# A hybrid decoder block on one core: the value part of its expert mixer written in program order on all engines, with new load rules, gather table and ending

## The chip, the core and the metric

The kernel runs on one core of a Trainium2 chip. The core has a matrix engine (TensorE, in the profile PE, with its weight loads as PEld), a vector engine (VectorE, DVE), a scalar engine (ScalarE, ACT), a general one (GpSimd, POOL), and a queue engine (SyncE, SP) that only issues transfers here. SP, ACT and POOL issue transfers, and 16 DMA engines carry them. The metric is the device time of one launch in microseconds, the median of several runs.

## The reference

One layer of a decoder for 512 tokens of width 1024: sliding-window attention beside gated linear attention, and then a channel mixer that picks, for each token and each of 8 heads, 16 of 16384 experts by product keys. The change lies in this mixer alone:

```python
def block(args):
    xb, eb, gb = args
    ub = jnp.take(u, eb, axis=0)
    hid = jax.nn.gelu(jnp.einsum('tkd,td->tk', ub, xb), approximate=False) * gb
    vb = jnp.take(v, eb, axis=0)
    return jnp.einsum('tk,tkd->td', hid, vb)
```

`u` and `v` are 16384 x 1024 in float32 each. The block's output is scaled by a row (gate 2), added to the residual, and a final RMS norm with a weight row follows.

## The kernel before

Of the four blocks of 128 tokens three (`DENSE`, 384 tokens) go through all experts: gelu(h u^T) for all 16384, times a dense matrix of gates that is zero where an expert was not picked, times v. (Of the third block's tokens 32 have their hidden values gathered; so the u side has 352 columns.) The experts lie in 128 chunks of 128. A float32 matmul is made of three (`mm3`, L69 to L72): each operand is split into a high part (a copy on ScalarE, L65) and a low part (a subtraction on VectorE, L66), by `hilo`. The fourth block (`GB`) gathers its rows: for each of 128 picks, `gather_u` gathers 128 rows of u (512 KB, an indirect transfer issued by GpSimd, L994) and takes their dot with the tokens on VectorE (L1004); `gather_v` gathers the rows of v (L1021) and adds them to `gacc` with the gelu'd, gated dot as weight (L1026). `gather_to` walks one list of 256 gathers, of which 24 dots are made earlier.

A **u chunk** (`u_part`, L693) is 24 matmuls of 352 columns and a gelu on ScalarE. 84 chunks (`AHEAD`: all even ones, and the odd ones from 89) are made before, while the gates are computed, and their gelus are spilled to DRAM (`gsp`). The other 44, odd, are made in the V part. A **v chunk** (`v_part`, L1165) takes a pair of chunks of v (1 MB for two), the gates of 8 chunks (`gr`, 1.5 MB from `Gd` in DRAM, one load for 8 chunks), the gelu (back from DRAM, `gel`, or from the odd u chunk), multiplies gates and gelu on VectorE (L1185), splits the product (`Ah` on ScalarE, L1189; `Al` on VectorE, L1190) and v (`vh`, `vl`), and adds 18 matmuls of 512 columns into six accumulators, two for each of the three blocks.

The loop of the V part goes over c from 0 to 123: at an even c the u chunk c + 9 (if it is not made ahead), then the v chunk, then as many gathers as a running share (4.0 for c in a pair with a u, 2.3 without) asks for, until c = 121. The last four chunks are multiplied block by block, and `finish` (L1202) multiplies a block by gate 2, adds the residual, squares it, makes the root (L80 to L87), scales and stores; for `GB` this is done at c = 123.

**What sets the order.** Instructions of an engine run in the order in which they are built. A list scheduler with an estimated timeline sets that order, unless an engine is under a manual schedule: then the order of the program stands. In the V part before, GpSimd alone is manual; VectorE, ScalarE, TensorE and SP are the scheduler's. Tiles come from pools of a fixed number of places (five `gr` and two `gr2` for gathers, four high and four low parts, four `Ah` and `Al`, three `raw`, two `vraw`, two for the gates), and an instruction that writes a place waits until its last reader is done.

Of the kernel before, what the change touches and what calls it, by code (L numbers as in the profile page):

```python
# [47 lines left out]
def peer_block_kernel(ctx: ExitStack, tc: tile.TileContext, a: dict, out: bass.AP):  # L48
# [951 lines left out]
    def gather_u(s):  # L1000
# [4 lines left out]
        if s % 8 == 7:  # L1005
            sl = slice(s - 7, s + 1)
            last_gelu["hg"] = nc.scalar.activation(hg[:, sl], hid[:, sl], AF.Gelu)
            waiting.append(sl)
# [149 lines left out]
    LAST = 4  # L1158

    def gates_of(j):  # L1160
        gates_of.next = dn.tile([P, NGRP, CG, TG], F32, tag="gring", bufs=2, name=f"gr{j}")
        load = (nc.sync if j else nc.gpsimd).dma_start(gates_of.next.rearrange("p g c t -> p g (c t)"), Gd[j])
# [155 lines left out]
```

## Time and profile before

| | us |
|---|---|
| median of 3 runs | 1521.37 (1520.15 to 1524.9) |
| profiled execution, its own time | 1526.09 |
| its span (first to last instruction) | 1524.3 |
| TensorE busy | 1447.2 (95%) |
| VectorE busy | 1265.6 (83%) |
| ScalarE busy | 676.5 (44%) |
| GpSimd busy | 502.3 (33%) |
| moved by DMA | 431.63 MB, mean 283 GB/s |

A row of a group of instructions names the line, the engine, the operation, what is written and read, the count, and then busy time, mean of one in ns, idle time before them and what ended it. A row of the timeline begins with the start in us and the duration. In a row of waits stand the waiter, what it waited for, and the sum in us, the number and the longest. Matmuls overlap, so that a row's duration is longer than the distance of two starts. The V part lies from 781 us to the end.

### The profile page before, as it was taken

The page shows a single profiled execution, that of the slowest core. Times are in us where ns is not written, and L with a number is a line of the kernel's source. Part 1 is how long each engine was busy: PE and PEld are TensorE (multiplying, and loading weights), DVE is VectorE, ACT ScalarE, POOL GpSimd, SP SyncE. Part 2 cuts the span into 40 slices and gives each one's busy share as a digit, 9 for nine tenths or more (in the row PEclk, how much of TensorE's full clock was granted, in tenths as well). Part 3 has the DMA queues.
Part 4 walks back from the last instruction along what each step waited for, and adds up shares of the span by engine and source line. Part 5 has one row for each costly group of instructions (what it writes and reads, how often), then busy time and mean ns, then how long its engine had stood idle before and what let it go on. Part 6 is the DMA issues. An engine that isn't in the chain of part 4 may idle for free. (4 is left out here: it accounts for less than half of the span.)

```text
span 1524.3 us, 24545 instructions
## 1 busy us (share of the span) xinstructions
PE 1447.2 (95%) x9387; PEld 1286.5 (84%) x9387; DVE 1265.6 (83%) x2421; ACT 676.5 (44%) x1072; POOL 502.3 (33%) x362
## 2 busy tenths in 40 slices
PE   3999999899999999999997999999999999998995
PEld 3787877788999999999996888888888888776774
DVE  7578757689999999799938878888788889897996
ACT  5455576533344555556633333333333333333333
POOL 1000000145506443032323344343443445554540
PEclk9999999999999999999998999999999999999998
DMA  9253435453347999799999999899998989999992
GB/s 347 99 208 111 169 98 206 148 191 111 138 163 242 325 360 349 243 319 330 316 352 404 380 357 344 311 334 357 347 339 320 345 311 344 392 403 406 373 347 88
DMA packets 165558, 431.63 MB, mean 283 GB/s; under 512 B 11856, under 2 KB 83568, under 8 KB 153024
## 3 DMA queue, kind: packets, MB, share of 16 engines
q1 hardware_dynamic: 109280, 259.88, 47.5%
q0 software_dynamic: 42000, 154.00, 27.1%
q10 hardware_dynamic: 14160, 16.19, 3.0%
q8 instruction: 73, 1.20, 0.3%
q14 instruction: 45, 0.37, 0.1%
HBM read 385.48 MB, written 44.50 MB: 282 GB/s over the span
## 5 line engine op out<-in xcount | busy, mean ns | idle before, releaser
L994 POOL DMA_INDIRECT gu<-in_u_dram,ix_u x128 | 181.7, 1420 | 281.6 <-DVE gacc L1026 104.1
L1021 POOL DMA_INDIRECT gv<-in_vP_dram,ix_v x128 | 172.8, 1350 | 209.6 <-DVE gu L1004 115.5
L1189 ACT ACTIVATE Ah<-gr 128x384 fp32r<-128x384 f32 x128 | 67.0, 525 | 336.7 <-PE acc L71 310.0
L1026 DVE SCALAR_TENSOR_TENSOR gacc<-gv,hg,gacc 128x1024 f32<-128x1024 f32 x127 | 162.7, 1281 | 0.9 <-DMA gv<-in_vP_dram,ix_v 0.7
L1004 DVE SCALAR_TENSOR_TENSOR gu<-gu,h2n 128x1024 f32<-128x1024 f32 x128 | 155.5, 1220 | 5.4 <-DMA gu<-in_u_dram,ix_u 5.2
L1190 DVE TENSOR_TENSOR Al<-gr,Ah 128x384 fp32r<-128x384 f32 x128 | 71.0, 557 | 51.7 <-ACT Ah L1189 49.0
L960 POOL DMA_INDIRECT spr<-in_u_dram,spix x32 | 72.5, 2266 | 104.9 <-DVE spr L965 67.8
L706 ACT ACTIVATE ge<-ph 128x352 f32<-128x352 f32 x128 | 57.8, 451 | 106.4 <-PE ph L72 106.4
L1076 POOL IOTA iot<- 128x256 bf16 x1 | 1.5, 1540 | 284.3 <-DVE h2Tl L681 284.3
L921 ACT ACTIVATE gs<-pg 128x512 f32<-128x512 f32 x96 | 95.2, 1116 | 0.0
L912 DVE TENSOR_TENSOR o<-o,gp 128x3072 bf16<-128x3072 bf16 x48 | 84.0, 1754 | 0.0
L919 PE MATMUL pg<-o,o 128*128 128x128 bf16 x1152 | 73.6, 219 | 0.0
L919 PEld LDWEIGHTS <-o 128*128 128x128 bf16 x1152 | 66.3, 97 | 5.4
L896 DVE TENSOR_TENSOR o<-iot,t 128x2048 bf16<-128x2048 bf16 x48 | 58.4, 1222 | 11.4 <-PE pg L919 11.4
L1185 DVE TENSOR_TENSOR gr<-gel,gr 128x352 f32<-128x352 f32 x84 | 39.7, 519 | 5.9 <-DMA gel<-gsp 5.9
L218 DVE SCALAR_TENSOR_TENSOR macc<-wa,scs,macc 128x1024 f32<-128x1024 f32 x28 | 39.3, 1403 | 4.4 <-DMA wa<-in_w_ada_dram 4.2
L965 DVE SCALAR_TENSOR_TENSOR spr<-spr,xs 128x1024 f32<-128x1024 f32 x32 | 39.1, 1221 | 2.3 <-DMA spr<-in_u_dram,spix 2.3
L1185 DVE TENSOR_TENSOR gr<-ge,gr 128x352 f32<-128x352 f32 x44 | 22.7, 522 | 21.6 <-DMA gr<-Gd 12.4
L71 PE MATMUL pq<-h2Tl,wq_0h 128*128 128x512 f32 (+1 forms) x80 | 27.9, 349 | 1.2 <-DVE h2Tl L681 1.2
L70 PE MATMUL pq<-h2Th,wq_0h 128*128 128x512 f32 (+1 forms) x80 | 28.0, 352 | 1.0 <-ACT qha L759 1.0
L71 PE MATMUL pq<-h2Tl,wq_1h 128*128 128x512 f32 (+1 forms) x80 | 28.1, 352 | 0.0
L72 PE MATMUL pq<-h2Th,wq_1l 128*128 128x512 f32 (+1 forms) x80 | 28.0, 350 | 0.0
(2610 smaller groups left out, 5029.5 us busy)
## 6 DMA issues: line engine op xcount, KB each, us to landing
u<-in_uT_dram SPq DMA_DIRECT2D x64, 1024.0 KB
v<-in_vP_dram SPq DMA_DIRECT2D x63, 1024.0 KB
Gd<-gs SPq DMA_DIRECT2D x23, 1024.0 KB
gr<-Gd SPq DMA_DIRECT2D x15, 1536.0 KB
wa<-in_w_ada_dram SPq DMA_DIRECT2D x20, 1024.0 KB
gsp<-ge ACTq DMA_DIRECT2D x84, 176.0 KB
gel<-gsp SPq DMA_DIRECT2D x41, 352.0 KB
wi<-in_w_in_dram SPq DMA_DIRECT2D x9, 1024.0 KB
```

The lines of the kernel that those rows point to most:

```text
L896: nc.vector.tensor_tensor(o12.rearrange("p g s k r -> p (g s) k r"), iot[:, None].to_broadcast([P, 2 * H, P, 2]), trs[n][0][:, g0:g0 + H]. ...
L912: nc.vector.tensor_tensor(o2, o12[:, :, 1, None].to_broadcast([P, H, 3, P, 2]), gp3[:, g0:g0 + H, :, None].to_broadcast([P, H, 3, P, 2]), ...
L919: nc.tensor.matmul(pt[:, i, :], o12[:, g, 0, :, r], o2[:, g, m, :, r], start=(m == 0), stop=(m == 2))
L921: nc.scalar.activation(gs[:, :, t0 + 4 * f:t0 + 4 * f + 4].rearrange("p b a -> p a b"), pt, AF.Copy)
L960: nc.gpsimd.indirect_dma_start(out=sp[j], out_offset=None, in_=a["u"], in_offset=bass.IndirectOffsetOnAxis(ap=sp["ix"][:, j:j + 1], axis=0))
L994: nc.gpsimd.indirect_dma_start(out=ur, out_offset=None, in_=a["u"], in_offset=bass.IndirectOffsetOnAxis(ap=ix_u[:, s:s + 1], axis=0))
L1004: nc.vector.scalar_tensor_tensor(ur, ur, 1.0, h2n, op0=OP.mult, op1=OP.mult, accum_out=hid[:, s:s + 1])
L1021: nc.gpsimd.indirect_dma_start(out=vr, out_offset=None, in_=a["vP"], in_offset=bass.IndirectOffsetOnAxis(ap=ix_v[:, s:s + 1], axis=0))
L1026: nc.vector.scalar_tensor_tensor(gacc, vr, hg[:, s:s + 1], gacc, op0=OP.mult, op1=OP.add)
L1185: nc.vector.tensor_tensor(A[:, :NGU], ge, A[:, :NGU], OP.mult)
L1189: nc.scalar.activation(grp(Ah), A, AF.Copy)
L1190: nc.vector.tensor_tensor(grp(Al), A, grp(Ah), OP.subtract)
```

## The change

All engines are under the manual schedule in the V part, and the V part is written anew around a list of steps `xs` (u chunks and v chunks, in the order in which TensorE takes them; a u chunk stands 8 or 9 chunks ahead of its v chunk, as before). `prep(i)` does what VectorE and ScalarE have to do for step i, and is called two steps ahead of the step's matmuls. The gathers stand inside `prep`, between the copies and the subtraction, by a table `due` that weighs each u step with 1.867 and each v step up to chunk 121 with 1.367. `loads(i)`, at the end of `prep(i)`, issues on SP each load whose place is free by then in program order and whose step is at most 9 to 12 ahead; when the u chunks are done, the three `raw` places serve v too. The first gates' load is split over SP and GpSimd, and v0 and its gelu move from GpSimd to SP. There are eight places for gathers instead of seven. The last four chunks are multiplied block by block, the first block by both halves together, and the ending of each block is split into halves that are interleaved. The dots' gelu moves behind the copies of a step. The number of matmuls and their forms stay, and everything ahead of the V part is built in the same order as before.

VectorE in the late part, around the subtraction for v chunk 100 (`vc100l`); `gu` and `gacc<-gv` are gathers, `Al` the low part of a gate product. Before:

```order
L1004 SCALAR_TENSOR_TENSOR gu112_13362,hid_2439<-gu112_13362,h2n_2430 128x1024
L1026 SCALAR_TENSOR_TENSOR gacc_8931<-gv95_13392,hg_2440,gacc_8931 128x1024
L1004 SCALAR_TENSOR_TENSOR gu113_13424,hid_2439<-gu113_13424,h2n_2430 128x1024
L1190 TENSOR_TENSOR Al102_13936<-gr12_13531,Ah102_13935 128x384
L1026 SCALAR_TENSOR_TENSOR gacc_8931<-gv96_13427,hg_2440,gacc_8931 128x1024
L1004 SCALAR_TENSOR_TENSOR gu114_13457,hid_2439<-gu114_13457,h2n_2430 128x1024
L1026 SCALAR_TENSOR_TENSOR gacc_8931<-gv97_13491,hg_2440,gacc_8931 128x1024
L1190 TENSOR_TENSOR Al103_13966<-gr12_13531,Ah103_13965 128x384
L1026 SCALAR_TENSOR_TENSOR gacc_8931<-gv98_13523,hg_2440,gacc_8931 128x1024
L66 TENSOR_TENSOR vc100l_13862<-v100_13859,vc100h_13861 128x1024
L66 TENSOR_TENSOR vc101l_13897<-v100_13859,vc101h_13896 128x1024
```

and now:

```order
L1289 TENSOR_TENSOR gr12_13422<-geo99_13523,gr12_13422 128x22x16
L1044 SCALAR_TENSOR_TENSOR gacc_8930<-gv104_13823,hg_2440,gacc_8930 128x1024
L1298 TENSOR_TENSOR vc99l_13817<-v98_13489,vc99h_13816 128x1024
L1302 TENSOR_TENSOR Al99_13821<-gr12_13422,Ah99_13820 128x384
L1289 TENSOR_TENSOR gr12_13422<-gel100_13654,gr12_13422 128x22x16
L1014 SCALAR_TENSOR_TENSOR gu121_13855,hid_2439<-gu121_13855,h2n_2430 128x1024
L1298 TENSOR_TENSOR vc100l_13849<-v100_13555,vc100h_13848 128x1024
L1302 TENSOR_TENSOR Al100_13853<-gr12_13422,Ah100_13852 128x384
L1289 TENSOR_TENSOR gr12_13422<-geo101_13590,gr12_13422 128x22x16
L1044 SCALAR_TENSOR_TENSOR gacc_8930<-gv105_13887,hg_2440,gacc_8930 128x1024
L1014 SCALAR_TENSOR_TENSOR gu122_13890,hid_2439<-gu122_13890,h2n_2430 128x1024
L1298 TENSOR_TENSOR vc101l_13881<-v100_13555,vc101h_13880 128x1024
```

Before, seven gathers stand between the subtractions of chunks 99 and 100, and the subtractions of four chunks follow each other; now one or two gathers stand in each step, and the list is thirteen gathers further on.

ScalarE at the start of the V part. Before:

```order
L706 ACTIVATE ge9_9091<-ph9_9066 128x352
L65 ACTIVATE vc0h_9097<-v0_9095 128x1024
L65 ACTIVATE vc1h_9133<-v0_9095 128x1024
L65 ACTIVATE uc11h_9166<-u9_9060 128x1024
L65 ACTIVATE vc2h_9199<-v2_9197 128x1024
L1189 ACTIVATE Ah0_9104<-gr0_9093 128x384
```

and now:

```order
L1290 ACTIVATE vc0h_9054<-v0_8949 128x1024
L1293 ACTIVATE Ah0_9058<-gr0_8946 128x384
L706 ACTIVATE ge7_9088<-ph7_9063 128x352
L1290 ACTIVATE vc1h_9090<-v0_8949 128x1024
L1293 ACTIVATE Ah1_9094<-gr0_8946 128x384
L706 ACTIVATE ge9_9126<-ph9_9101 128x352
L1284 ACTIVATE uc11h_9128<-u9_8935 128x1024
```

TensorE takes u11 ahead of v0 before, and v0 and v1 ahead of u11 now; the copies follow that.

SP at the same place (`gr0` are the first gates, `gr1` the next). Before:

```order
L698 DMA u9_9060<-in_uT_dram 128x2048
L1171 DMA v2_9197<-in_vP_dram 128x2x1024
L1171 DMA v4_9298<-in_vP_dram 128x2x1024
L1162 DMA gr1_9300<-Gd_2438 128x3072
L1180 DMA gel4_9306<-gsp_2437 128x2x352
```

and now:

```order
L1215 DMA u9_8935<-in_uT_dram 128x2048
L1242 DMA gr0_8946<-Gd_2438 64x3072
L1221 DMA v0_8949<-in_vP_dram 128x2x1024
L1227 DMA gel0_8951<-gsp_2437 128x2x352
L1221 DMA v2_8953<-in_vP_dram 128x2x1024
L1221 DMA v4_8955<-in_vP_dram 128x2x1024
```

The loads of v2 and v4 stood ahead of any load of gates, and now stand behind the first gates, v0 and its gelu.

The core of the diff:

```diff
-GR = 5
+GR, G2 = 5, 3
...
-    dve_s.close()
-    ctx.enter_context(tc.manual_schedule(engines={mybir.EngineType.Pool}))
+    ctx.enter_context(tc.manual_schedule(engines={mybir.EngineType.PE, mybir.EngineType.Activation, mybir.EngineType.SP}))
...
+    LEAD, LAST, LAST_G = 8, 4, 121
+    rest = [c for c in range(1, P, 2) if c not in AHEAD]
+    xs = [("u", c) for c in rest if c <= LEAD]
+    for c in range(0, P, 2):
+        if c + 1 + LEAD in rest:
+            xs.append(("u", c + 1 + LEAD))
+        xs += [("v", c), ("v", c + 1)]
+    step = {x: i for i, x in enumerate(xs)}
+    first_v, last_g = step["v", 0], step["v", LAST_G]
+    rate = {"u": (0.385 * 3.84 - 0.5) / 0.524, "v": (0.385 * 4.146 - 0.88) / 0.524}
+    share = [rate[k] if first_v + 2 <= i <= last_g else 0 for i, (k, c) in enumerate(xs)]
+    due = [EARLY + int((len(gathers) - EARLY) * sum(share[:i + 1]) / sum(share) + 1e-6) for i in range(len(xs))]
...
+    class Ring:
+        def __init__(self, make, bufs):
+            self.make, self.bufs, self.freed = make, bufs, []
+        def free(self, i):
+            return len(self.freed) < self.bufs or self.freed[-self.bufs] <= i
+        def take(self, name, freed):
+            self.freed.append(freed)
+            return self.make(name)
+    raws = Ring(lambda name: raw([P, 2, D], name), 3)
+    vraws = Ring(lambda name: dn.tile([P, 2, D], F32, tag="vraw", bufs=2, name=name), 2)
...
+    def load_v(ring):
+        c = vrest.pop(0)
+        v = ring.take(f"v{c}", step["v", c + 1])
+        nc.sync.dma_start(v, vPc[c:c + 2].rearrange("c i d -> i c d"))
+        vraw[c], vraw[c + 1] = v[:, 0], v[:, 1]
...
+    def load_gates():
+        j = jrest.pop(0)
+        t = gates_r[j] = grs.take(f"gr{j}", step["v", j * CG + CG - 1])
+        flat = lambda h: t[h].rearrange("p g c t -> p g (c t)")
+        if j == 0:
+            for h, eng in ((slice(0, 64), nc.sync), (slice(64, P), nc.gpsimd)):
+                eng.dma_start(flat(h), Gd[j, h])
...
+    def loads(i):
+        at = lambda x, n: step[x] <= i + n
+        if i == 1:
+            load_gates()
+            load_v(raws)
+            load_gel()
+        if i < 1:
+            return
+        while True:
+            if vrest and at(("v", vrest[0]), 12) and vraws.free(i):
+                load_v(vraws)
+            elif vrest and not urest and at(("v", vrest[0]), 9) and raws.free(i):
+                load_v(raws)
+            elif urest and at(("u", urest[0]), 9) and raws.free(i):
+                load_u()
+            elif grest and at(("v", grest[0]), 9) and gels.free(i):
+                load_gel()
+            elif orest and at(("v", orest[0]), 9) and odds.free(i):
+                load_odd()
+            elif jrest and at(("v", jrest[0] * CG), 11) and grs.free(i):
+                load_gates()
...
+    def close_half(n, src, q):
+        y, xr, ss = fin[n][:3]
+        nc.vector.tensor_tensor(half(y, q), src, half(gate2b, q), OP.mult)
+        nc.vector.tensor_tensor(half(y, q), half(y, q), half(xr, q), OP.add)
+        nc.scalar.activation(half(xr, q), half(y, q), AF.Square, accum_out=ss[:, q:q + 1])
...
+    def prep(i, extra=()):
+        k, c = xs[i]
+        weigh()
+        if k == "u":
+            src = uraw.pop(c)
+            h, l = halves([P, KD, P], f"uc{c}")
+            nc.scalar.activation(h, src, AF.Copy)
+        else:
+            src = vraw.pop(c)
+            h, l = halves([P, D], f"vc{c}")
+            A = gates_r[c // CG][:, :, c % CG, :]
+            nc.vector.tensor_tensor(A[:, :NGU], (gel if c % 2 == 0 else ges).pop(c), A[:, :NGU], OP.mult)
+            nc.scalar.activation(h, src, AF.Copy)
+            Ah = dn.tile([P, TD], FR, tag="Ah", bufs=4, name=f"Ah{c}")
+            Al = dn.tile([P, TD], FR, tag="Al", bufs=4, name=f"Al{c}")
+            nc.scalar.activation(grp(Ah), A, AF.Copy)
+        activate()
+        gather_to(due[i])
+        for piece in extra:
+            piece()
+        nc.vector.tensor_tensor(l, src, h, OP.subtract)
+        if k == "u":
+            ready[i] = h, l
+        else:
+            nc.vector.tensor_tensor(grp(Al), A, grp(Ah), OP.subtract)
+            ready[i] = c, Ah, Al, h, l
+        loads(i)
...
+    extras = {
+        step["v", LAST_G - 4]: [gate2_rows],
+        step["v", LAST_G + 1]: [table],
+        step["v", LAST_G + 2]: [lambda: [close_half(GB, half(gacc, q), q) for q in range(2)]],
+        step["v", LAST_G + 3]: [lambda: root(GB)],
+        step["v", LAST_G + 4]: [lambda: refine(GB), lambda: finish(GB)],
+    }
+    load_u()
+    load_u()
+    load_u()
+    end = step["v", P - LAST]
+    prep(0)
+    prep(1)
+    for i in range(end):
+        if i + 2 < len(xs):
+            prep(i + 2, extras.get(i + 2, ()))
+        k, c = xs[i]
+        if i == step["v", LAST_G - 4]:
+            gate2_sums()
+        if i == step["v", 16]:
+            bcast_load(fwb, a["fw"], D)
+        if k == "u":
+            phs[c] = u_matmuls(c, *ready.pop(i))[0]
+            u_gelu(c, phs.pop(c))
+            odds.freed.append(step["v", c])
+            rest_u.discard(c)
+        else:
+            v_matmuls([ready.pop(i)])
+    for i in range(end + 2, len(xs)):
+        prep(i, extras.get(i, ()))
+    last = [ready.pop(i) for i in range(end, len(xs))]
+    v_matmuls(last[:3], (0,))
+    v_matmuls(last[3:], (0,))
+    for b in DENSE[1:]:
+        for q in range(2):
+            v_matmuls(last, (b,), (q,))
+    n0, n1, n2 = DENSE
+    x0, x1 = fin[n0], fin[n1]
+    for n, y, xr in ((n0, spare("y0"), x0), (n1, spare2("y1"), x1)):
+        fin[n] = [y, xr, dn.tile([P, 5], F32, tag=f"sm{n}", bufs=1, name=f"sm{n}")]
+    open_block(n2, spare2("y2"), spare("xf2"))
+    w2 = spare("w2")
+    close_half(n0, acc[0], 0)
+    close_half(n0, acc[1], 1)
+    close_half(n1, acc[2], 0)
+    root(n0)
+    refine(n0)
+    finish(n0)
+    close_half(n1, acc[3], 1)
+    close_half(n2, acc[4], 0)
+    root(n1)
+    refine(n1)
+    y1, r1 = fin[n1][0], fin[n1][4]
+    for q in range(2):
+        nc.scalar.activation(half(y1, q), half(y1, q), AF.Copy, scale=r1)
+        nc.gpsimd.tensor_tensor(half(y1, q), half(y1, q), half(fwb, q), OP.mult)
+        store(n1, q, y1)
+    y2 = fin[n2][0]
+    nc.vector.tensor_tensor(half(w2, 0), half(y2, 0), half(fwb, 0), OP.mult)
+    close_half(n2, acc[5], 1)
+    nc.vector.tensor_tensor(half(w2, 1), half(y2, 1), half(fwb, 1), OP.mult)
+    root(n2)
+    refine(n2)
+    r2 = fin[n2][4]
+    nc.scalar.activation(half(w2, 0), half(w2, 0), AF.Copy, scale=r2)
+    store(n2, 0, w2, nc.scalar)
+    nc.vector.tensor_scalar(half(w2, 1), half(w2, 1), r2, None, op0=OP.mult)
+    store(n2, 1, w2)
```

More of the change, by code (lines that the diff above doesn't have):

```diff
@@ L710, in u_part @@
             ges[c] = ge
+    def u_part(c, lo_eng=None, after=None):
+        j = c // 2 % 2
+        if j == 0:
+            u_load(c)
+        uh, ul = hilo(u_part.raw[c % 2][:, j], [P, KD, P], f"uc{c}", lo_eng or nc.vector)
+        with tc.issue_after(after.ins) if after is not None else nullcontext():
+            ph, end = u_matmuls(c, uh, ul)
+        u_gelu(c, ph)
         return end
@@ L1224, in peer_block_kernel @@
-    LEAD, LAST_G = 8, 122
-    share = [4.0 if c + 1 + LEAD < P and c + 1 + LEAD not in AHEAD else 2.3 for c in range(0, P, 2)]
-    cost = [share[c // 2] for c in range(LAST_G)]
-    for c in range(1, 1 + LEAD, 2):
-        u_part(c)
-    for c in range(P - LAST):
-        if c % 2 == 0 and c + 1 + LEAD < P and c + 1 + LEAD not in AHEAD:
-            u_part(c + 1 + LEAD)
-        with tc.issue_after(last_gelu["u"].ins) if c < 2 else nullcontext():
-            parts = v_part(c)
-        v_matmuls([parts])
-        weigh()
-        gather_to(EARLY + int((len(gathers) - EARLY) * sum(cost[:c + 1]) / sum(cost) + 1e-6))
-        if c == LAST_G + 1:
-            with tc.issue_after(last_gelu["u"].ins), tc.issue_after(last_gelu["hg"].ins):
-                nc.scalar.preload_act_table_set("natural_log_exp_and_others")
-            finish(GB, [gacc[:, 0:512], gacc[:, 512:1024]])
-        if c == 16:
-            tc.keep_in_program_order(bcast_load(fwb, a["fw"], D))
-        if c == P - 16:
-            dg = gp.tile([P, KD, P], F32, tag="gr", bufs=GR, name="dg")
-            nc.vector.tensor_tensor(dg, ident[:, None, :].to_broadcast([P, KD, P]),
-                                    modT[:, 40:48, None].to_broadcast([P, KD, P]), OP.mult)
-            for q in range(2):
-                pb = pbank(f"g2b{q}")
-                for i in range(4):
-                    nc.tensor.matmul(pb[:, i * P:(i + 1) * P], ones, dg[:, 4 * q + i, :], start=True, stop=True)
-                nc.scalar.activation(h2n[:, q * 512:(q + 1) * 512], pb, AF.Copy)
@@ new lines, in gate2_sums, with table @@
+    def gate2_sums():
+        assert all(f is gather_v for f, s in gathers[gather_to.n:])
+        for q in range(2):
+            pb = pbank(f"g2b{q}")
+            for i in range(4):
+                nc.tensor.matmul(pb[:, i * P:(i + 1) * P], ones, gate2_rows.dg[:, 4 * q + i, :], start=True, stop=True)
+            nc.scalar.activation(half(gate2b, q), pb, AF.Copy)
+    def table():
+        assert weigh.n == NS and not rest_u
+        nc.scalar.preload_act_table_set("natural_log_exp_and_others")
+        open_block(GB, spare("y3"), spare("xf3"))
+        for n in DENSE[:2]:
+            fin[n] = spare(f"xf{n}")
+            nc.sync.dma_start(fin[n], x1d[n])
```

159 lines of the change are left out of this document (87 added, 72 removed).

## Prediction

> **What bounds the kernel now.** I read the stretches of the last half first (each row: length, then busy time and instructions of TensorE, its weight loads, VectorE, ScalarE and GpSimd, granted clock, DMA share, GB/s), then TensorE's waits, then single rows.
>
> ```profile
> 781.00:800.70 19.70, 19.67 (x122) 19.08 (x120) 2.98 (x4) 4.21 (x7) 7.18 (x9) 1.00 0.92 338
> 800.70:831.90 31.20, 23.02 (x97) 19.72 (x98) 26.59 (x40) 12.01 (x18) 9.23 (x9) 0.84 1.03 406
> 831.90:1280.20 448.30, 448.30 (x2245) 395.84 (x2244) 370.93 (x481) 164.20 (x233) 198.07 (x143) 1.00 0.91 339
> 1280.20:1320.00 39.80, 39.80 (x178) 32.96 (x177) 34.03 (x48) 11.84 (x17) 20.46 (x15) 1.00 1.02 402
> 1320.00:1460.00 140.00, 126.23 (x535) 101.35 (x534) 127.70 (x176) 48.70 (x68) 74.14 (x55) 0.96 1.00 385
> 1460.00:1507.20 47.20, 47.14 (x208) 38.66 (x206) 42.01 (x54) 15.45 (x28) 8.96 (x8) 1.00 0.66 244
> 1507.20:1524.30 17.10, 0.00 (x0) 0.00 (x0) 8.08 (x25) 4.49 (x15) 3.24 (x2) 0.60 0.25 92
> ```
>
> TensorE sets the end in the V part: from 831.9 to 1320 it never rests. It rests at 800.7 to 831.9, in 1320 to 1460, and it has finished 17 us before the end. How much of this is loss needs the price of its work: in the long stretch the first matmuls of uc13 and uc87 stand 37 groups (two v chunks, one u chunk) apart, and the rows of uc7 and uc9 give a u chunk.
>
> ```profile
> L70 PE MATMUL ph<-h2Th,uc13h x8: 321/323/325, 831.9 to 835.2; 128*128 128x352 f32 x8
> L70 PE MATMUL ph<-h2Th,uc87h x8: 321/323/325, 1276.4 to 1279.7; 128*128 128x352 f32 x8
> 792.86 0.32 PE L70 MATMUL ph<-h2Th,uc7h 128*128 128x352 f32 x1
> 796.70 0.32 PE L70 MATMUL ph<-h2Th,uc9h 128*128 128x352 f32 x1
> 781.03 0.32 PE L70 MATMUL ph<-h2Th,uc1h 128*128 128x352 f32 x1
> 1451.85 1.95 PE L1251 MATMUL g2b<-dg,ones 128*128 128x128 f32 x16
> 1506.76 0.39 PE L72 MATMUL acc<-vc127h,Al 128*128 128x512 f32 x1
> ```
>
> (1276.4 - 831.9)/37 = 12.01 us a group, 796.70 - 792.86 = 3.84 a u chunk, so (12.01 - 3.84)/2 = 4.085 a v chunk. The work from 781.03 on is 44 x 3.84 + 128 x 4.085 + 1.95 = 693.8 us, and would end at 1474.8. It ends at 1506.76 + 0.39 = 1507.15: **32.3 us are lost on TensorE**. u11 and v0 to v3 (3.84 + 4 x 4.085 = 20.2) could start at 781.03 + 5 x 3.84 = 800.2 and end at 820.4, but uc13 starts at 831.9: the start loses 11.4, and the rest 20.9. The waits say for what:
>
> ```profile
> PE ph L70 <- ACT uc11h L65: 7.5, 1, 7.5
> PE acc L71 <- DVE vc104l L66: 3.1, 1, 3.1
> ...
> PE acc L71 <- DVE vc108l L66: 0.3, 1, 0.3
> ```
>
> Eleven waits, 21.7 us together; the other 10 or so are matmuls at a lower clock behind them (0.84 in the second row of stretches). All the late waits name chunks from 88 to 116, each a multiple of four.
>
> **The start.**
>
> ```profile
> 772.53 1.34 SPq L1171 DMA_DIRECT2D v<-in_vP_dram  x2
> 787.96 0.34 SPq L1162 DMA_DIRECT2D gr<-Gd  x1
> 788.49 0.58 POOL L1162 DMA_DIRECT2D gr<-Gd  x1 [25.49 <-DMA gsp<-ge]
> 800.17 2.27 DVE L1185 TENSOR_TENSOR gr<-ge,gr 128x352 f32<-128x352 f32 x5 [12.36 <-DMA gr<-Gd]
> 805.20 1.06 ACT L65 ACTIVATE vc0h<-v 128x1024 fp32r<-128x1024 f32 x1 [4.00 <-DMA v<-in_vP_dram]
> 808.20 0.66 PE L70 MATMUL ph<-h2Th,uc11h 128*128 128x352 f32 x1 [7.50 <-ACT uc11h L65]
> ```
>
> uc11's copy stands behind vc0 and vc1 on ScalarE, vc0 waits for v0, and v0 was issued on GpSimd behind the first gates (gr0), which wait for the last gates' store. TensorE needs v0 and gr0 some 3 us ahead of 800.2 (copy 1.06, gate product, two subtractions); they came at 800.2 and 805.2. Now: the two early loads (v2, v4; 2.1 MB) that shared the transfers with that store stand behind gr0. At 338 GB/s they are worth 6 us, so gr0 can go between 782 and 788; I take 784. Of what follows, SP carries half of gr0, v0 and gel0, 0.79 + 1.05 + 0.36 = 2.2 MB; if GpSimd's half and its gathers take half of 406 GB/s, that is 10.8 us: 794.8, and 799 from the late end. Loss at the start from 0 to 11.4 (all as before); I take 2, near the low end because the middle case is 2.5 us early.
>
> **The late stretch.** VectorE has no slack there (127.7 of 140 busy), and its order is in clumps. The change spreads it; what a step costs VectorE comes from starts that follow each other:
>
> ```profile
> 1326.39 1.22 DVE L1004 SCALAR_TENSOR_TENSOR gu<-gu,h2n 128x1024 f32<-128x1024 f32 x1
> 1327.54 1.28 DVE L1026 SCALAR_TENSOR_TENSOR gacc<-gv,hg,gacc 128x1024 f32<-128x1024 f32 x1
> 1328.73 1.22 DVE L66 TENSOR_TENSOR vc90l<-v,vc90h 128x1024 fp32r<-128x1024 f32 x1
> 1329.87 1.22 DVE L66 TENSOR_TENSOR vc91l<-v,vc91h 128x1024 fp32r<-128x1024 f32 x1
> 812.85 1.96 DVE L1190 TENSOR_TENSOR Al<-gr,Ah 128x384 fp32r<-128x384 f32 x4
> L1026 DVE SCALAR_TENSOR_TENSOR gacc<-gv,hg,gacc 128x1024 f32<-128x1024 f32 x75 | 96.1, 1281 | 0.0
> L1004 DVE SCALAR_TENSOR_TENSOR gu<-gu,h2n 128x1024 f32<-128x1024 f32 x69 | 84.0, 1218 | 0.0
> ```
>
> A u gather takes 1.15, a v gather 1.19 (1.17 mean), a subtraction of 1024 columns 1.14, the Al 1.96/4 = 0.49, the gate product 2.27/5 = 0.45. The last two rows are of 831.9 to 1280.2: 144 gathers in 37 groups, 3.9 a group. The code of before plans 4.46 there; the order that was built let them slip, so too many fell behind 1280. By the new table a group gets 4.5 and a v chunk without a u 1.34 (232 gathers over 39 u and 120 v steps, weights 1.867 and 1.367, times 0.98). VectorE then needs 3 x 1.14 + 2 x 0.45 + 2 x 0.49 + 4.5 x 1.17 = 10.6 of 12.01 us a group, and 1.14 + 0.45 + 0.49 + 1.34 x 1.17 = 3.65 of 4.085 in a late chunk: 88 and 89%. The moved gathers lie beside matmuls that take longer, and ScalarE (164 of 448 us) and GpSimd (198) have room. Wait added: a gather's dot now stands ahead of its chunk's subtraction, and behind it everything of the next steps; two prepared chunks (8 us) cover it.
>
> The transfers must carry it too. From the tiles' sizes a group takes 0.52 (u) + 1.05 (v) + 0.39 (gates) + 0.18 (gelu) + 4.5 x 0.524 = 4.5 MB in 12.01 us, 375 GB/s, and a late chunk 0.52 + 0.20 + 0.18 + 0.70 = 1.60 MB in 4.085, 392 GB/s, against 402 over 40 us and 406 over 31 us above. That is tight: loss between 0 (402 and 488 us without a rest) and 20.9 (as before); at the 385 of the stalling stretch 42 late chunks lose (1.60/0.385 - 4.085) x 42 = 3 us. I take 3.
>
> [...]
>
> **The end.** Block by block, v127 must be ready when TensorE has done 18 matmuls of the last four chunks (18 x 4.085/18 = 4.1 us) instead of 12; its copy can start when v123 is through, and takes 1.06 + 0.53 (Ah) + 1.14 + 0.49 = 3.2: no wait. Behind the last matmul before:
>
> ```profile
> 1507.73 0.68 DVE L1210 TENSOR_TENSOR y<-acc,h2n 128x512 f32<-128x512 f32 x1
> 1509.72 0.63 ACT L1212 ACTIVATE xl<-y 128x512 f32<-128x512 f32 x1
> 1511.87 0.15 DVE L81 TENSOR_SCALAR rf2m<-ssf 128x1 f32<-128x1 f32 x1
> 1513.10 0.16 DVE L87 TENSOR_TENSOR rf2y<-rf2y,rf2t 128x1 f32<-128x1 f32 x1
> 1512.79 1.33 ACT L1218 ACTIVATE y<-y,rf1y 128x512 f32<-128x512 f32 x2 [0.29 <-DVE rf1y L87]
> 1515.14 1.70 POOL L1219 TENSOR_TENSOR y<-y,fwb 128x512 f32<-128x512 f32 x1
> ```
>
> All three blocks were completed together; the last product ended at 1515.14 + 1.70 = 1516.84, 9.7 us after TensorE. Now block 0 is complete 10.9 us and block 1 some 5.4 us ahead of the end. At TensorE's end VectorE still has block 1's root and a product of block 2 (2 us by these rows); then two half products (1.3), the square (0.8), sum and root (0.3 + 1.4), one half scaling (0.7): 6.5 us, 3.2 less. From there to the end of the span lie 1524.3 - 1516.84 = 7.5 us, kept.
>
> **The sum.** 1474.8 + 2 + 3 + 6.5 + 7.5 = 1493.8 us of span, 30.5 less. The profiled execution took 1526.09 for a span of 1524.3, and the median is 1521.37, 0.3% under it: (1493.8 + 1.8) x 1521.37/1526.09 = **1491 us**, 2.0% less. With both losses at 0 it is 1486, with 14 us of them 1500.
>
> **Rivals.**
>
> *The waits stay in part* (1502). Gates late at the start (8) and gathers bunched behind a burst of loads (8): 11 us more. For it: SP and GpSimd carry all loads in order, and transfers are at 0.91 to 1.03 of their share throughout. Against it: the new table has no clumps.
>
> *VectorE becomes the bound, slower* (1533). In the late part it has 4.085 - 3.65 = 0.43 us a step, 0.32 a gather. If each of the 232 gathers kept it waiting 0.5 us at its fixed place, they would add (0.5 - 0.32) x 232 = 42 us. From 0.32 + 30.5/232 = 0.45 us a gather on nothing is won. Against it is how seldom before, with seven places, it waited for them in the whole V part:
>
> ```profile
> DVE gu L1004 <- DMA gu<-in_u_dram,ix_u: 1.9, 3, 0.9
> DVE gacc L1026 <- DMA gv<-in_vP_dram,ix_v: 0.7, 1, 0.7
> ```
>
> 2.6 us of 232 gathers; for it, that gathers landed early while VectorE was late. With eight places a gather has 8 x 4.085/1.34 = 24 us from the place's release to its next use.
>
> *The transfers are the bound* (1529).
>
> ```profile
> 500.00:550.00 50.00, 50.00 (x434) 49.05 (x434) 49.30 (x53) 29.44 (x40) 21.71 (x13) 1.00 1.02 357
> ```
>
> Here a full share of 1.02 moved only 357 GB/s. With that as ceiling a group takes 4.5/0.357 = 12.6 (0.6 x 39 = 24 us more) and a late chunk 4.49 (0.4 x 42 = 17): 41 instead of the 3 above, 38 more. Against it: that stretch stores gates in pieces of 512 bytes, the V part does not. [...]
>
> **How the numbers follow.** Forecast 0.66 (1486 to 1500 by itself), waits stay in part 0.22, VectorE 0.06, transfers 0.06. The last two have a third to a half of their weight within 0.3% of 1521 (what a measurement here can tell from no change), as their price may be less: faster 0.88, same 0.05, slower 0.07. The range is 1482 (losses at 0, end shorter) to 1512 (26 us of losses), which leaves out the last two and the worst of the second.
>
> **What would show it.** Right: TensorE from 781 to some 1480 with under 8 us of waits, uc13's place taken by v0 close to 800, 15 gathers per 40 us before 1270 and 13 after, DMA at 365 to 395 GB/s without a stretch under 340, VectorE's idle time split over all steps, the last store within 7 us of the last matmul. Wrong: waits of VectorE on gu or gv above 50 us in all, matmuls waiting on a subtraction every few chunks, or a start at which vc0 again waits beyond 805.

## The result, and the profile after

| | before | after |
|---|---|---|
| median of the runs side by side, us | 1523.13 (1520.15 to 1525.77) | 1507.39 (1503.95 to 1509.21) |
| ratio | | 0.9895, 95% interval 0.9866 to 0.9923 |
| profiled execution, its own time | 1526.09 | 1503.95 |
| its span | 1524.3 | 1502.2 |

The change gains 1.05%, about half of the 2.0% forecast, and the time lies in the forecast's range. First the stretches of the V part after, cut where its steps change (length, then busy time and instructions of TensorE, its weight loads, VectorE, ScalarE and GpSimd, granted clock, DMA share, GB/s):

```profile
778.50:822.40 43.90, 42.09 (x218) 37.71 (x217) 24.37 (x32) 16.10 (x23) 19.46 (x16) 0.96 0.99 354
822.40:1274.80 452.40, 452.40 (x2221) 392.06 (x2220) 394.03 (x518) 166.30 (x232) 259.76 (x168) 1.00 0.97 376
1274.80:1320.00 45.20, 45.20 (x203) 37.11 (x202) 41.85 (x60) 17.00 (x24) 23.37 (x16) 1.00 1.03 408
1320.00:1440.00 120.00, 120.00 (x516) 96.54 (x515) 106.15 (x140) 42.93 (x60) 44.52 (x34) 1.00 0.99 378
1440.00:1490.40 50.40, 50.40 (x226) 40.85 (x224) 35.99 (x62) 19.75 (x39) 0.00 (x0) 1.00 0.23 81
1490.40:1502.20 11.80, 0.00 (x1) 0.00 (x0) 6.23 (x15) 3.32 (x8) 2.94 (x2) 0.65 0.24 89
```

From 822.4 to the last matmul TensorE is never idle, at a clock of 1.00, and the DMA carries 376 to 408 GB/s until GpSimd has issued its last gather. The waits that the change was to remove are gone. What is left of them in the V part, on TensorE one, and the longest of VectorE:

```profile
PE acc L70 <- ACT Ah L1293: 1.7, 1, 1.7
DVE gr L1289 <- DMA gel<-gsp: 9.4, 1, 9.4
```

1.7 us for 21.7, and yet only half of the gain. A TensorE without a rest tells nothing of how fast it works. The group interval does, read as in the prediction from the first matmuls of uc13 and uc87:

```profile
L70 PE MATMUL ph<-h2Th,uc13h x8: 321/322/323, 822.4 to 825.8; 128*128 128x352 f32 x8
L70 PE MATMUL ph<-h2Th,uc87h x8: 321/321/323, 1274.8 to 1278.2; 128*128 128x352 f32 x8
```

(1274.8 - 822.4)/37 = 12.23 us a group, where it was 12.01. The u matmuls keep their 160.0 ns from start to start, so it is the v chunks. Of one chunk behind the last u, the six matmuls of L70, every third of its 18 (count, shortest, median and longest duration in ns, first and last start), in the kernel before:

```profile
L70 PE MATMUL acc<-vc80h,Ah x6: 389/389/389, 1288.4 to 1291.8; 128*128 128x512 f32 x6
```

and after:

```profile
L70 PE MATMUL acc<-vc80h,Ah x6: 392/395/398, 1287.0 to 1290.5; 128*128 128x512 f32 x6
L72 PE MATMUL acc<-vc80h,Al x6: 392/395/398, 1287.5 to 1291.0; 128*128 128x512 f32 x6
```

From the first to the last start are 15 matmuls: (1291.8 - 1288.4)/15 = 0.2267 us each before, (1290.5 - 1287.0)/15 = 0.2333 after. The starts in the trace say 226.7 and 233.3 ns, before in an even beat, after in turns of 229 and 237.5. All chunks of the changed kernel are slow (means of 232.0 to 233.6 ns within a chunk, v0 with its wait and v117 behind the gate 2 matmuls left out), at 376 GB/s and more and also in the last 50 us, at 81 GB/s. 128 x 18 x 6.6 ns = **15.2 us**: the missing half. In the stretches above, TensorE takes this time as work: 100% busy at a clock of 1.00.

By the terms of the forecast, all from the profiled executions:

| | forecast | after |
|---|---|---|
| V part starts | 781.0 | 778.5 |
| from there to the end of the last matmul | 693.8 + 5 = 698.8 | 711.9 |
| from there to the end of the span | 14.0 | 11.8 |
| span | 1493.8 | 1502.2 |

The order of matmuls within a normal chunk, their form and the bytes that they read are the same in both kernels. What could make each one 3% slower? Two theories were tried. (An address here is the byte at which a tile begins in each of its 128 partitions, or rows.) **A, addresses**: the change lays the pool of the V part (`dn`) anew (a third gather place, fewer gelu places, other small tiles), which moves the weights Ah and Al from byte 189408 and 195552 of a partition to 204640 and 210784; the halves of v stay at 88032 + 4096 n. **B, a pattern**: weight loads and matmuls fall into one of several repeating beats, and the stalls of the kernel before happened to start the good one.

### The profile page after: what moved, and what is told of

It reads as the page before. It is cut to its first block, busy times and chain, and to the rows that moved or that the text cites. A ratio compares the mean times of both kernels' runs of the same rounds, so it can differ in the third digit from the quotient of the medians.

```text
span 1502.2 us, 24546 instructions
## 1 busy us (share of the span) xinstructions
PE 1451.1 (97%) x9387; PEld 1281.2 (85%) x9387; DVE 1262.3 (84%) x2422; ACT 681.3 (45%) x1073; POOL 533.8 (36%) x360
## 4 chain that ended last, share of the span: by engine, by line
PE 90%; DVE 4%; ACT 3%; DMA 2%; issue 1%; SPq 0%; DVEq 0%; ACTq 0%
PE acc L71 12%; PE acc L72 12%; PE acc L70 12%; PE ph L70 10%; PE ph L72 10%; PE ph L71 10%; PE pg L929 4%; PE pq L70 2%; PE pq L72 2%; PE pq L71 2%; DMA gel<-gsp 1%; PE pj L72 1%; PE pj L70 1%; PE pj L71 1%; DVE macc L275 1%; PE pn L70 1%
## 5 line engine op out<-in xcount | busy, mean ns | idle before, releaser
L1004 POOL DMA_INDIRECT gu<-in_u_dram,ix_u x128 | 197.1, 1540 | 252.5 <-DVE gu L1014 103.8
L1039 POOL DMA_INDIRECT gv<-in_vP_dram,ix_v x128 | 190.6, 1489 | 177.2 <-DVE gacc L1044 112.1
L1289 DVE TENSOR_TENSOR gr<-gel,gr 128x352 f32<-128x352 f32 x64 | 33.2, 519 | 9.4 <-DMA gel<-gsp 9.4
L70 PE MATMUL pq<-h2Th,wq_0h 128*128 128x512 f32 (+1 forms) x80 | 28.0, 352 | 1.0 <-ACT qha L769 1.0
L70 PE MATMUL pq<-h2Th,wq_1h 128*128 128x512 f32 (+1 forms) x80 | 28.0, 349 | 0.0
```

Source lines behind the costliest of these rows:

```text
L70: nc.tensor.matmul(acc, lh, rh, start=start, stop=False)
L1004: nc.gpsimd.indirect_dma_start(out=ur, out_offset=None, in_=a["u"], in_offset=bass.IndirectOffsetOnAxis(ap=ix_u[:, s:s + 1], axis=0))
L1039: nc.gpsimd.indirect_dma_start(out=vr, out_offset=None, in_=a["vP"], in_offset=bass.IndirectOffsetOnAxis(ap=ix_v[:, s:s + 1], axis=0))
```

## The experiments

**The old addresses, and a control.** The first run lays the tiles of the pool where they were; that needs the room of the third gather place, so the control takes this away too and nothing else.

```diff
-GR, G2 = 5, 3
+GR, G2 = 5, 2
...
     gacc = dn.tile([P, D], F32, name="gacc")
+    order_of = [("gring", [P, NGRP, CG, TG], F32, 2), ("gel", [P, 2, TU], F32, 2), ("Ah", [P, TD], FR, 4),
+                ("Al", [P, TD], FR, 4), ("vraw", [P, 2, D], F32, 2), ("gr2", [P, D], F32, G2), ("pad", [P, 736], F32, 1)]
+    for tag, shape, kind, n in order_of:
+        dn.tile(shape, kind, tag=tag, bufs=n, name=f"at_{tag}")
```

> The changed kernel with seven gather places, and with every tile of the V part's pool laid at the address that it had in the kernel before (Ah at 189408 for 204640, Al at 195552 for 210784). In the changed kernel a 128x512 matmul of the V part starts 233.3 ns after the one before it, in the kernel before 226.7 ns. Theory A, it is the address of the weights that the loads read: spacing back at 226.7 ns, 128 chunks x 18 matmuls x 6.6 ns = 15 us less than the run with seven places and the new addresses, so about 1493 us where that is at 1508. Theory B, weight loads and matmuls lock into one of several repeating patterns, chosen by what happened before: spacing at 233 ns as before, and no difference between these two runs beyond 3 us.

> The changed kernel with seven gather places (the third place of the second pool taken away), which moves that pool's tiles by 4096 bytes and nothing else. Both theories on the matmuls: 233 ns stays (A: 4096 bytes is a whole number of all the small units; B: nothing disturbs). The eighth place: if the gathers need it, VectorE waits for gathered rows where it waited 12 us in all with eight, and the time rises by up to 5 us; if not, 1507 us.

Measured: 1491.44 us (ratio 0.9786, 0.9752 to 0.9821) at the old addresses, 1504.82 (0.988, 0.9843 to 0.9918) in the control. A chunk of the first, and of the second:

```profile
L70 PE MATMUL acc<-vc85h,Ah x6: 389/389/389, 1299.7 to 1303.1; 128*128 128x512 f32 x6
```

```profile
L70 PE MATMUL acc<-vc85h,Ah x6: 392/395/398, 1307.8 to 1311.3; 128*128 128x512 f32 x6
```

226.7 and 233.3 ns, with the same instructions. Theory A stands, and the time is the forecast's 1491. The control also says what the eighth gather place is worth: nothing that can be measured (1504.82 against 1507.39, intervals overlapping). The 12 us of waits in its expectation are not all for gathered rows: 9.4 are for the gelu shown above, 2.8 for rows of u.

**Other orders.** This was to find a stretch that leaves the slow beat by itself, as B would have it.

```diff
+            if c == 24 or 48 <= c < 88:
+                one = lambda i, q, x, y: nc.tensor.matmul(acc[2 * i + q], x[:, i * P:(i + 1) * P],
+                                                          y[:, q * 512:(q + 1) * 512], start=False, stop=False)
...
```

> The changed kernel with the 18 matmuls of a chunk in other orders in parts of the V part: chunk 24 alone, and chunks 48 to 71, with the six products of Ah and the high half first and then the other twelve in turns; chunks 72 to 87 with the products of one weight slice side by side (two per weight); all others as in the changed kernel. The same products are summed. Theory A (addresses): 233.3 ns wherever the old order stands, 25 to 47 and 88 to 115 included, since the addresses are those of the changed kernel. Theory B (a pattern chosen by history): the spacing of the chunks behind chunk 24 or behind chunk 87 may differ from 233.3 ns though order and addresses there are unchanged, and goes on so until the next disturbance; if all the stretches got 226.7 ns, 128 x 18 x 6.6 = 15 us less, and each stretch in proportion. If an order of itself costs, chunks 48 to 71 or 72 to 87 alone differ.

1507.58 us (0.9893, 0.9861 to 0.9925). One chunk with the six products of Ah first (L1309 is the line of the new orders; six starts in a row here), one with two products per weight, one of the old order behind it all:

```profile
L1309 PE MATMUL acc<-vc49h,Ah x6: 392/395/398, 1105.7 to 1106.9; 128*128 128x512 f32 x6
L1309 PE MATMUL acc<-vc73h,Ah x6: 392/395/398, 1252.4 to 1255.5; 128*128 128x512 f32 x6
L70 PE MATMUL acc<-vc90h,Ah x6: 392/395/398, 1335.3 to 1338.8; 128*128 128x512 f32 x6
```

The mean spacing is 233.1 ns in chunks 4 to 23 and 25 to 47, 233.1 in 48 to 71, 233.2 in 72 to 87, 233.3 in 88 to 115. Neither an order nor a disturbance gets out of the slow beat. B is out as the cause.

**The repair in one line.** If the remainder by 512 bytes or less is what counts, 128 bytes are enough: 189408 = 369 x 512 + 480 and 204640 = 399 x 512 + 352. The four small tiles of the ending take 32 bytes each. Laid first, they move everything behind them by 128.

```diff
     gacc = dn.tile([P, D], F32, name="gacc")
+    small = [dn.tile([P, 5], F32, tag=f"sm{n}", bufs=1, name=f"sm{n}") for n in range(NT)]
...
-        fin[n] = [y, xr, dn.tile([P, 5], F32, tag=f"sm{n}", bufs=1, name=f"sm{n}")]
+        fin[n] = [y, xr, small[n]]
```

> The changed kernel, eight places and all, with one difference: the four small tiles of 32 bytes (the sums of the last step) are laid ahead of the big tiles of their pool and not behind them, which moves Ah and Al by 128 bytes, from 204640 and 210784 to 204768 and 210912. Theory A (the address of the weights sets the matmul's spacing, and what counts is its remainder in units of 512 bytes or less: 480 in the kernel before, 352 in the changed one): spacing 226.7 ns, about 1491 us. Theory A' (what counted in the run with the old addresses is the whole address or its place in a larger unit, or another tile): spacing stays 233 ns, 1505 to 1508 us. The eighth place against the run with seven at the old addresses (1491.4): within 3 us either way.

**1491.26 us** (1489.54 to 1492.84; ratio 0.9796, 0.9776 to 0.9816): 2.0% faster than the kernel before and 16 us faster than the changed one. The stretches of this run:

```profile
779.60:798.80 19.20, 19.20 (x122) 19.09 (x120) 2.45 (x2) 4.81 (x7) 8.41 (x9) 1.00 0.94 284
798.80:823.20 24.40, 22.60 (x98) 18.60 (x97) 21.63 (x30) 11.29 (x16) 10.71 (x7) 0.93 1.02 412
823.20:1267.70 444.50, 444.50 (x2221) 392.03 (x2220) 393.84 (x518) 166.40 (x232) 257.75 (x168) 1.00 0.98 383
1267.70:1320.00 52.30, 52.30 (x239) 43.97 (x238) 49.38 (x70) 20.08 (x28) 28.27 (x19) 1.00 1.03 406
1320.00:1440.00 120.00, 120.00 (x540) 99.64 (x539) 107.75 (x140) 44.00 (x62) 41.18 (x32) 1.00 0.97 376
1440.00:1477.60 37.60, 37.52 (x166) 30.75 (x164) 26.99 (x52) 15.63 (x32) 0.00 (x0) 1.00 0.12 42
1477.60:1489.50 11.90, 0.00 (x0) 0.00 (x0) 6.23 (x15) 3.42 (x9) 2.94 (x2) 0.67 0.24 88
```

(1267.7 - 823.2)/37 = 12.01 us a group, and in the 120 us from 1320 TensorE makes 540 matmuls instead of 516. From the first matmul of the V part to the last are 697.9 us, where the forecast had 698.8.

**The kernel before, 128 bytes further.** The reverse: an unused piece of 128 bytes in the kernel before.

```diff
+    dn.tile([P, 32], F32, name="gap")
     xl = dn.tile([P, 2, D], F32, tag="vraw", bufs=2, name="xl")
```

> The kernel before with 128 unused bytes at the end of the V part's pool, which moves Ah and Al from the remainder 480 to 352 by 512 bytes, and its other tiles too; order and waits as written stay. Theory A: spacing 233 ns, TensorE's work in the V part grows by 128 x 18 x 6.6 ns = 15 us; as 21.7 us of its time there are waits for VectorE, which a slower TensorE makes shorter, the time grows by 5 to 15 us, to 1528 to 1538 us. Theory A' (another cause): spacing 226.7 ns and 1523 us.

1532.21 us, ratio 1.0066 (1.0043 to 1.0089), and the slow beat:

```profile
L70 PE MATMUL acc<-vc81h,Ah x6: 392/395/398, 1305.1 to 1308.6; 128*128 128x512 f32 x6
```

So the slowness has nothing to do with the changed order: it is there in the old program too. In the profiled execution the V part grows from 726.1 to 733.7 us, by half of the 15: TensorE's wait for vc104l, 3.1 us, is gone, and so is the stretch of 6.8 us at a granted clock of 0.50 that began in it, at 1398.1 us, and cost 3.4. What the slower matmuls cost here, 7.6 us for 15, hung on how much TensorE had waited. (The expectation calls the 21.7 us waits for VectorE; by their names 17.2 are for ScalarE's copies and 4.5 for VectorE's subtractions.)

**Which distance.** Two single executions put the four places of Ah and Al at other remainders, by chunk: 4n, 4n+1, 4n+2, 4n+3.

```diff
+    for k, gap in enumerate((0, 256, 192, 32)):
+        if gap:
+            dn.tile([P, gap // 4], F32, tag=f"gap{k}", bufs=1, name=f"gap{k}")
+        for h in ("Ah", "Al"):
+            dn.tile([P, TD], FR, tag=f"{h}{k}", bufs=1, name=f"{h}first{k}")
+    dn.tile([P, 416 // 4], F32, tag="rest", bufs=1, name="rest_gap")
...
-            Ah = dn.tile([P, TD], FR, tag="Ah", bufs=4, name=f"Ah{c}")
+            Ah = dn.tile([P, TD], FR, tag=f"Ah{c % 4}", bufs=1, name=f"Ah{c}")
```

(The second has gaps of 0, 32, 32, 64 and 224 at the end; Al as Ah.)

> The changed kernel with seven places and the four places of Ah and Al at four remainders by 512 bytes: 480, 224, 416 and 448 for the chunks 4n, 4n+1, 4n+2 and 4n+3. Known so far: 480 goes with 226.7 ns a matmul, 352 with 233.3. If units of 256 bytes decide, 224 is as fast as 480, and 416 and 448 may be slow; if units of 128 bytes decided, 352 would have been fast, so that is out; if only the fit with the other operand's place decides (the halves of v lie at 480), 480 alone is fast and 224, 416 and 448 are slow; if the chunk before sets the pattern more than the address, all four show one spacing.

> As the run with four remainders, with the places of Ah and Al for the chunks 4n, 4n+1, 4n+2 and 4n+3 at 0, 32, 64 and 128 by 512 bytes: 32, 64, 96 and 160 bytes past those of the halves of v, where the earlier runs had 0 (226.7 ns), -256 (226.7), -128 (233.3), -32 (233) and -64 (226 to 232, mixed). If only a distance of whole 256 bytes is fast, all four chunks are above 228 ns and the time is 1500 to 1508 us, with 160 bytes (the same as -96 by 256) no better than the others. If some other distance is as fast, its chunk shows 227 ns; one under 226 ns would mean that the old places were not the best.

1498.93 and 1508.17 us. Chunks 80 to 83 of the first (0, -256, -64 and -32 bytes from the remainder of v's halves):

```profile
L70 PE MATMUL acc<-vc80h,Ah x6: 389/391/397, 1284.7 to 1288.1; 128*128 128x512 f32 x6
L70 PE MATMUL acc<-vc81h,Ah x6: 389/389/389, 1288.8 to 1292.2; 128*128 128x512 f32 x6
L70 PE MATMUL acc<-vc82h,Ah x6: 392/392/392, 1292.9 to 1296.3; 128*128 128x512 f32 x6
L70 PE MATMUL acc<-vc83h,Ah x6: 393/395/397, 1297.0 to 1300.5; 128*128 128x512 f32 x6
```

and chunks 84 to 87 of the second (32, 64, 96 and 160 bytes):

```profile
L70 PE MATMUL acc<-vc84h,Ah x6: 395/396/396, 1307.3 to 1310.8; 128*128 128x512 f32 x6
L70 PE MATMUL acc<-vc85h,Ah x6: 394/394/396, 1311.5 to 1315.0; 128*128 128x512 f32 x6
L70 PE MATMUL acc<-vc86h,Ah x6: 391/394/400, 1315.7 to 1319.2; 128*128 128x512 f32 x6
L70 PE MATMUL acc<-vc87h,Ah x6: 394/394/402, 1319.9 to 1323.4; 128*128 128x512 f32 x6
```

Where all six last 389 ns the spacing is 226.7 ns; longer and mixed durations (up to 402 ns) go with a slower one, 228.5 to 234.1 ns. Mean spacing over the chunks 80 to 115, with the earlier runs:

| distance of weights and halves of v, bytes modulo 256 | 0 | 32 | 64 | 96 | 128 | 160 | 192 | 224 |
|---|---|---|---|---|---|---|---|---|
| ns from start to start | 226.7 | 233.3 | 233.4 | 233.6 | 233.3 | 234.1 | 229.1 | 233.4 |

(0 from the kernel before and the runs at the old or repaired places, 128 from the changed kernel, both with the steps from chunk to chunk; within a chunk 128 has 233.6. -256 had 226.6. Right behind a slow chunk a chunk at distance 0 begins with some eight uneven starts before the even beat, 228.5 ns on average.) Of the tried distances only a whole number of 256 bytes is fast: 226.6 and 226.7 ns, where the seven others have 229.1 to 234.1.

**Both operands moved.** Is it the place of the weights, or its fit with the other operand? Here the weights keep their slow place (352), and the halves of v come to 352 as well.

```diff
-GR, G2 = 5, 3
+GR, G2 = 5, 2
...
+    h2p.tile([P, 96], F32, name="gap")
     hl = ctx.enter_context(tc.tile_pool(name="hl", bufs=1, side="left", reuse_waits="tile"))
```

> The changed kernel with seven places, Ah and Al at the remainder 352 by 512 bytes where their matmuls take 233.3 ns, and the halves of v (and of u) moved by 384 bytes, so that they have the remainder 352 as well. If the matmul is slow because its two operands lie differently, it is back at 226.7 ns here and the time is about 1491 us; if it is the place of the weights alone, 233 ns and 1503 to 1508 us. The u chunks, whose weights move here, show whether their 160.0 ns hold.

```profile
L70 PE MATMUL acc<-vc84h,Ah x6: 389/389/389, 1302.4 to 1305.8; 128*128 128x512 f32 x6
```

226.7 ns with the weights at a place that was slow in the changed kernel: it is the distance. The single execution took 1498.03 us, 7 above the expected 1491. Its V part is short (699.9 us); it starts at 784.1 and not at 779.6, in work that lies ahead of the change; the other runs of the changed kernel named here start it between 777.3 and 784.3. The u matmul, whose two operands lay 192 bytes apart by 256 and lie 64 apart here, went from 160.0 to 160.5 ns.

**The u matmuls at distance 0.**

```diff
-GR, G2 = 5, 3
+GR, G2 = 5, 2
...
+    h2p.tile([P, 48], F32, name="gap0")
     h2Th = h2p.tile([P, KD, T], FR, name="h2Th")
...
+    h2p.tile([P, 16], F32, name="gap1")
     hl = ctx.enter_context(tc.tile_pool(name="hl", bufs=1, side="left", reuse_waits="tile"))
```

(with the small tiles first)

> The run with the small tiles first (1491.3 us), with seven places (which cost nothing at the old addresses: 1491.4 us) and two unused pieces of 192 and 64 bytes ahead of and behind h2Th and h2Tl. The u chunks' two operands, 192 bytes apart by 512 until now, come to a distance of whole 256 bytes, as those of the v chunks have and keep. The u matmul (128x352) starts 160.0 ns after the one before it. [...] Theory two, the distance slows u as well: under 158 ns, and 128 chunks x 24 matmuls x 2 ns = 6 us or more.

1491.8 us (0.9789, 0.9754 to 0.9824): no change that can be measured. In the V part the u matmuls now start every 161.0 ns (under 158 in theory two), where it was 160.0, in an uneven beat of 156 to 165 ns. Ahead of it, where u chunks follow each other, the repaired run and this one have 160.0 to 160.3, this one mostly an even 160. So what the v matmuls show does not hold for every matmul: the u matmuls stay within 1 ns at the distances 0, 64 and 192 (161.0, 160.5 and 160.0 ns), and 0 is not their best; the v matmuls lose 6.7 ns at 64 and 2.4 at 192. Whether the number of columns makes the difference is not shown. The operands differ too (the halves of u are the weights and the tokens move), and the distance of 128 was not tried on u.

**One step ahead instead of two**, with the matmuls at 233 ns and at 226.7 ns.

```diff
     prep(0)
-    prep(1)
     for i in range(end):
-        if i + 2 < len(xs):
-            prep(i + 2, extras.get(i + 2, ()))
+        if i + 1 < len(xs):
+            prep(i + 1, extras.get(i + 1, ()))
```

> The changed kernel with groups prepared one ahead and not two; program order, loads, last chunks and eight places stay. If the lead of two is what removed TensorE's waits (21.7 us in the kernel before, 2 us now), they come back in part, 5 to 20 us, and the time is 1512 to 1525 us; if program order alone removed them, TensorE waits under 5 us and the time stays within 4 us of 1507. For the matmul spacing theory B allows another value after each such wait, theory A does not: 233.3 ns throughout.

> The run with the small tiles first (1491.3 us), with groups prepared one ahead. At the slow matmuls a lead of one cost nothing (1506.6 against 1507.4 us). At 226.7 ns a matmul TensorE leaves VectorE 0.5 us less a group, and the lead may matter: if VectorE's share of 88 to 89% is room enough, within 3 us of 1491; if the lead is what covers its uneven load, waits of 1 to 3 us at ten or more chunks, 1496 to 1510.

1506.61 us (0.9885, 0.9852 to 0.9917) and 1493.58 (0.9798, 0.9768 to 0.9828), against 1507.39 and 1491.26. In both TensorE waits once in the V part, in the second so:

```profile
PE acc L70 <- ACT Ah L1294: 3.5, 1, 3.5
```

That is 1.8 us more than with two, at the start, and nothing behind it; the intervals do not tell the times apart. So the lead of two is not what removed the waits.

**The scheduler's order on the other engines.** Only VectorE and GpSimd keep the program's order.

```diff
-    ctx.enter_context(tc.manual_schedule(engines={mybir.EngineType.PE, mybir.EngineType.Activation, mybir.EngineType.SP}))
```

(with the small tiles first)

> The run with the small tiles first (1491.3 us), with the order of TensorE, ScalarE and the loads in the V part left to the scheduler, as in the kernel before; VectorE and GpSimd keep the program's order, and lead, places and last chunks stay. If TensorE's waits went because VectorE's order is the program's, this run keeps them away and is within 4 us of 1491. If the order of the other three engines is what counts, waits come back, 5 to 25 us, and the time is 1496 to 1516.

1506.99 us (0.99, 0.9868 to 0.9932). The time is in the range of the second theory, but not for its reason: TensorE's only wait of the V part is one of 3.5 us, and the V part takes 699.8 us (697.9). Of the 13.6 us by which the profiled span is longer, 11.8 are lost behind the last matmul, in 23.8 us instead of 12.0:

```profile
L1341 ACT ACT_TABLE_LOAD x4 | 5.1, 1283 | 0.1
L1342 ACT ACT_TABLE_LOAD x4 | 5.1, 1283 | 0.1
DVE sm L1348 <- ACT sm L1342: 11.7, 4, 3.6
```

Each of the four roots loads ScalarE's tables twice, 8 x 1.28 us, and VectorE waits 11.7 us for the roots; three of the four stand behind the last matmul. With the program's order there is one load in the ending, ahead of all roots:

```profile
1442.38 1.28 ACT L1378 ACT_TABLE_LOAD   x1
```

So TensorE's waits stay away without the program's order on TensorE, ScalarE and SP. Of the orders, VectorE's is the one left that can have removed them; the new places and load rules stayed in all runs and were not tried apart from it. In the ending the program's order on ScalarE keeps out the seven further table loads; the kernel before had one load as well (1.28 us at 1453.56), so this is not what shortened the ending.

## Why the prediction was wrong, step by step

**The bound** (TensorE in the V part; 32.3 us lost): right. Every run that did away with the waits shortened the V part, and no other engine or transfer took over. The reading of the late waits is right in part only. Of their 13.5 us, 9.7 name ScalarE's copies of v, and the prediction speaks of VectorE's clumps alone. Chunk 88 in the kernel before:

```profile
PE acc L70 <- ACT vc88h L65: 1.7, 1, 1.7
1321.00 0.52 ACT L1189 ACTIVATE Ah<-gr 128x384 fp32r<-128x384 f32 x1 [3.56 <-PE acc L71]
1321.73 0.21 ACT L1007 ACTIVATE hg<-hid 128x8 f32<-128x8 f32 x1 [0.21 <-DVE gu L1004]
1321.85 1.04 ACT L65 ACTIVATE vc88h<-v 128x1024 fp32r<-128x1024 f32 x1
```

The copy stood in ScalarE's order behind one that waited 3.56 us for TensorE and one that waited for a gather's dot on VectorE. How much belongs to which engine's order stays open.

**The price of the work: here it failed.** The step was "128 x 4.085 ... = 693.8", a v chunk's price measured before and carried over as if it belonged to the chunk. It belongs to the chunk and to the distance of its two operands. The step that the prediction did not make was to ask what, beside the order, the change does to the tiles that the matmuls read: the third gather place and the other tile sizes move Ah and Al by 15232 bytes = 59 x 256 + 128. After the change a chunk takes (12.23 - 3.84)/2 = 4.195 us; 128 x (4.195 - 4.085) = 14.1 us, just the difference of the V part (711.9 - 697.9 = 14.0). With the old distance the same change gives 1491.26 and 1491.44, the forecast's 1491. That it fits to the microsecond is luck: the repaired run's span is 4.3 us under the forecast's 1493.8 (1.4 earlier at the start of the V part, 0.9 less lost in it, 2.0 less at the end), and the 4.6 us that the forecast took off because the profiled execution before lay above its median were not there (this run's profiled execution, 1491.26, is the median).

**The start** (loss of 2 instead of 11.4): better than before, but twice the forecast. v0's first matmul came at 799.6 (forecast close to 800). In the repaired run the V part's loss is 697.9 - 693.8 = 4.1 us, forecast 2 + 3 with the late stretch, and all of it lies at the start: up to uc13 are 823.2 - 779.6 = 43.6 us for 19.2 + 20.2 = 39.4 us of work. 1.7 of it is the one wait, and 1.7 more the clock of 0.93 in the second stretch (24.4 x 0.07 = 1.7); the rest stays open.

**The late stretch** (loss of 3): no loss at all, which makes up for the start in the sum. VectorE at 393.84/444.5 = 89% in the long part (forecast 88), 49.38/52.3 = 94% then and 107.75/120 = 90% late (89). DMA 383 GB/s where 375 were asked, 406 and 376 late (392).

**The end**: 12.0 for 14.0. The last product ended 7.4 us after TensorE (forecast 6.5), but from there to the end of the span are 4.5 us and not the 7.5 of before:

```profile
1484.49 0.48 DVE L1453 TENSOR_SCALAR w<-w,sm 128x512 f32<-128x512 f32 x1
1485.00 0.33 SPq L1355 DMA_DIRECT2D out_dram<-w  x1
```

**The rivals.** "The waits stay in part" gave 1502 and the time came out near it, at 1507, with 1.7 us of waits: right in size for a wrong reason, as the stretches show. VectorE as the bound: after the change it waited 2.8 us in all for gathered rows of u. The transfers: 408 GB/s over 45 us, above the 357 of this rival.

**The signs named.** v0 at 799.6, waits under 8 us, and 168 gathers of GpSimd in 452.4 us, 14.9 per 40 us (15), are as named; from there to 1440 they are 50 in 165.2 us, 12.1 (13). Two are not: the first 20 us carried 284 GB/s in the repaired run and 286 in the changed one (no stretch under 340 was named), and the last store was issued 7.3 us after the last matmul (7). None of the signs was the speed of a matmul, so they could not show this error.

## What to carry to other kernels

An engine that is always busy can still be slow (here, 100% busy at a clock of 1.00 in the 120 us from 1320, 516 matmuls against 540 after the repair): after every change, compare the start-to-start time of the bounding instruction with the one before, not only its busy share. Where it differs for the same instruction, look at the addresses of its operands, which any new buffer, pad or small tile in the same pool can move; for the 128x512 float32 matmuls here a distance of a whole multiple of 256 bytes between weights and moving operand is worth 3% (226.7 ns from start to start for 233.3 at 128 bytes), and putting four small tiles first got it back. A price measured in one layout holds for that layout: a v chunk took 4.085 us in the one and 4.195 in the other.

## What the hardware showed that was not expected

The spacing of the v matmuls, with weights of 128x128 and 512 moving columns of four bytes, goes with where their two operands lie to each other: 226.7 ns at a distance of 0 modulo 256 bytes, 229.1 to 234.1 ns at seven other distances in steps of 32. The longer spacing is a repeating beat (at 128 bytes 229 and 237.5 ns in turns, or a longer cycle of 228 to 241 after a disturbance), and it was there at 378 GB/s of transfers as at 81. Tiles moved by 128 bytes were enough to change it both ways: from 226.7 to 233.3 ns in the kernel before, from 233.3 to 226.7 in the changed one. What lies behind it, and why the u matmuls with their 352 columns lose at most 1 ns, was not measured and stays open.
